# A two-layer decoder trunk on one core: score products over all 128 rows, value products and compression alternating between two column halves

## The chip, the core and the metric

The kernel runs on one core of one Trainium2 chip. The metric is the device time of one execution in microseconds (us). The median of three runs of the kernel before is 717.5 us (716.52 to 721.53).

## What is computed

There are two layers over 256 tokens of width 1024, all in float32. Cut to what matters here, a layer is:

```
h   = RMSNorm(x);  p = h @ W_in                 # one projection, columns split among three groups of heads
o_A = HGRN2 gated linear recurrence             # 4 heads, state 64x64
o_B = gate0*softmax(q.kc)vc + gate1*softmax(q.ks)vs + gate2*softmax(q.kw)vw    # 8 heads of 64, 2 groups of keys
      kc, vc = gelu(flat(32-token blocks of k, v) @ w1) @ w2                   # 15 compressed keys and values a group
o_C = softmax(q.k + c_q - c_k) v                # forgetting attention, 4 heads of 64; c = running sum of log f
x   = x + concat(o_A, o_B, o_C) @ W_o
x   = x + relu(RMSNorm(x) @ W_up)^2 @ W_down
```

With 256 tokens, the selected branch (ks, vs) and the window branch (kw, vw) of B each see every key up to the query's position.

## The kernel before, in words

Every weight matrix streams through one DMA queue (SyncE's, SP) in tiles of 128 x 1024 values (512 KB). `load` (L207) puts a tile into one of five `raw` buffers. `load_split` (L212) divides it into two exact float32r parts: ScalarE (ACT) writes `whi` (L219), VectorE (DVE) writes `wlo = raw - whi` (L220). `mm3` (L223) makes one exact product of three float32r products on TensorE (PE), L225 to L227. The projection of W_in, the output projection W_o and the MLP use it; they are most of PE's work.

Between W_in and W_o stand the three groups of heads. A token tile t is 128 tokens.

- **Scores of B** (`head_b`, L804). For each head and token tile two products are summed in a bank `sc`: L813 over 128 rows (rows 0-63 the hi part of q against the hi part of k, rows 64-127 the lo part of q against hi of k), and L814 over rows 0-63 only (hi of q against `KLB`, the lo part of k). `KLB` is the lower half of a tile `KLO`; 256 columns for tile 0, 512 for tile 1. 8 heads x 2 tiles x 2 layers give 32 such pairs. The softmax follows: DVE masks and takes the maximum (L743), ACT exponentiates (L161), DVE and ACT scale (L751, L749), PE transposes (L828, L833), ACT copies to SBUF (L830, L835).
- **Scores of C** (`head_c`, L858). Per token tile three products: L867 over 128 rows, L868 over rows 64-127 (`KLC`, the upper half of `KLO`), and L869 over the two rows 32h and 32h+1 (`ones_r` against `CC`, which holds the running sums). 4 heads x 2 tiles x 2 layers give 16 such triples.
- **Value products of B** (`pv_b`, L838). One bank takes two heads: head e = 0 writes partitions 0-63 (columns 0-63 of the array), head e = 1 partitions 64-127. All four products of the first head come first, then all four of the second, between two full-width products with the compressed values (`cmp_out`, L842). L850 has 256 columns, L852 has 128. These operands are plain float32, and the trace shows each such product as two passes. There are four per layer. `pv_c` (L883) does the same for C with two products a head.
- **Compression** (`b_compress`, L597). The first product of the compressed keys (w = 0) and values (w = 1): 35 output rows, 128 columns, 16 steps each. Steps w0 and w1 of the order do the keys, w2 and w3 the values, each with its own 512 KB `raw` tile, which is used as loaded and so stays held until the step's last product. Both results stand on partitions 0-34, in different columns.

`ORDER` (L54) writes out the steps of a layer by hand. The framework's scheduler then merges them into a stream per engine, and decides when a tile gets a buffer that is free. PE, DVE, ACT and SP each run their stream in order; an instruction that waits holds up all behind it. The steps that the prediction speaks of are these:

```
"t2", "t3", "vg", "b2", "b1", "w0", "t4", "w1", "cv", "+ai", "w2", "w3", "ai", "t5", "kc", "b0", "+q1", "q1", ...
... "b4", "b5", "b6", "c0", "pb2", "b7", "pb3", "c1", "wo0", "pc0", "wo1", "c3", "wo2", "c2", "pc1", "wo3"
```

Here `b` is head_b, `c` head_c, `w` b_compress, `pb` pv_b, `pc` pv_c, `kc` the rest of the compression, `t` a level of A (L466 on PE, then L475 to L486 on DVE), `+q1` the projection of a chunk and `wo` tiles of the output projection.

Of the kernel before, what the change touches and what calls it, by code (L numbers as in the profile page):

```python
# [10 lines left out]
F32 = mybir.dt.float32  # L11
F32R = mybir.dt.float32r
# [6 lines left out]
P = 128  # L19
# [13 lines left out]
# Column chunks of w_in, in the order in which they are projected.  # L33
# (name, list of (first column, end column))
# [16 lines left out]
# The first three chunks are projected together, token tile 0 first; then the steps of a layer up to the output projection, in the  # L51
# order in which they are issued ("+" marks the projection of a chunk, its bare name the use of the result).
# [6 lines left out]
# Parts of the probabilities that ScalarE scales (0-3: of B, 4-5: of C); VectorE scales the others.  # L59
# buffers of weight tiles: as loaded, their hi parts, their lo parts  # L60
WBUFS = (5, 6, 5)
# [9 lines left out]
# Columns of the constant table.  # L71
# [12 lines left out]
# Columns of the per-layer table of small parameters.  # L84
V_BQG = 0      # per-partition gain of the B queries (1 on the rotary dims)
# [3 lines left out]
V_POS = 4      # [kv, 16]  # L89
# [5 lines left out]
V_LB = V_FB + 4   # [pair, layer]  # L95
V_G2 = V_LB + 4    # per K-tile
# [39 lines left out]
def tile_block(ctx: ExitStack, tc: tile.TileContext, x_in, win, wo, wup, wdn, w1, vec, cst, out, dbg=None):  # L136
# [4 lines left out]
    # One table set holds every activation used here.  # L141
# [13 lines left out]
    def act_exp(*a, **k):  # L155
        """Exp and Ln come from the set loaded last; they stay behind its load."""
        if after[0] is None:
            r = A.activation(*a, **k)
        else:
            with tc.issue_after(after[0]):  # L160
                r = A.activation(*a, **k)  # L161
        last_exp[0] = r.ins
        return r

    def act_sigmoid(*a, **k):
        """Sigmoid comes from another set: behind every Exp and Ln issued so far."""
# [18 lines left out]
    # ---- tiles that live through the whole kernel  # L185
# [6 lines left out]
    ones_r = T([P, P], F32R, tag="ones_r", pool=cpool)  # L192
# [4 lines left out]
    KLO = T([P, 1024], F32R, tag="KLO", pool=cpool)  # L197
# [4 lines left out]
    for z in (Qbd, AT, LF, hidT, KC.bitcast(F32), VC.bitcast(F32), PCS.bitcast(F32)):  # L202
        G.memset(z, 0.0)
    KLB = KLO[0:64, :].rearrange("p (g n) -> p g n", g=2)
    KLC = KLO[64:128, :].rearrange("p (h t) -> p h t", h=4)

# [5 lines left out]
    def load_split(src, n, parts=1):  # L212
        """Loads [128, n] of weights; gives exact float32r parts hi and lo, worked out in so many parts."""
# [23 lines left out]
    def rsqrt(ss, n, a, b, parts=P, st="n", out=None, rms=None):  # L237
        """(a * ss + b) ** -0.5 on [parts, n], with one Newton step. With rms, ss is of unscaled values of both
        token tiles, a names the column of a * r^2, and the result is multiplied by r."""
# [21 lines left out]
    def norm_stats(t):  # L261
        """mean(x^2) + eps of the tokens of tile t."""
# [19 lines left out]
    def kt_split():  # L282
        """Exact parts hi and lo of a [1024, 256] operand, feature-major, four K-tiles a tile."""
        return [[T([P, 4, S], F32R, "kt4", 6) for _ in range(2)] for _ in range(2)]

    def kt_parts(a, k, sl):
        """hi and lo of K-tile k, columns sl."""
# [4 lines left out]
    def gain_splits(a, ks, sl, ps, vt, v0):  # L292
        """K-tiles ks of a, columns sl, from what stands side by side in ps, times their gains."""
# [8 lines left out]
    def begin(L):  # L302
        """Tiles of a layer's start: parameters, x * g1 feature-major, 1 / rms of x, the first tile of w_in."""
# [6 lines left out]
        rms = T([P, 2, 4], tag="rms", bufs=1)    # per token tile: r, r^2, r^2 / DH, -r  # L310
# [3 lines left out]
    def norm1(st, t):  # L314
        """x * g1 of the tokens of tile t, feature-major; 1 / rms goes on what the projections give."""
# [21 lines left out]
    for L in range(DEPTH):  # L337
# [10 lines left out]
        def proj_tok(name):  # L348
            """Token-major projection of 256 columns: one bank, [token tile, 256]."""
# [6 lines left out]
        def proj_feat(name):  # L356
            """Feature-major projection of 256 columns: one bank, [column block, 256 tokens]."""
# [763 lines left out]
```

## Time and profile before

| | us |
|---|---|
| median of the runs shown | 717.5 |
| span of the profiled execution | 715.8 |
| PE busy in the span | 705.0 |
| DVE busy | 453.3 |
| ACT busy | 398.5 |
| POOL (GpSimd) busy | 8.3 |

The profiled execution is listed by its span alone, 715.8 us from its first to its last instruction; the runs' median lies 1.7 us above it, with what stands around the span. L12 is line 12 of the kernel. PEld are the weight loads that overlap products. A product's own time includes its way through the array, so consecutive products overlap in the listing, and what one costs in a stream is the distance from its start to the next start. A wait that is hidden in such an overlapped row is not listed as idle.

### The profile page before, as it was taken

The page shows a single profiled execution, that of the slowest core. Times are in us where ns is not written, and L with a number is a line of the kernel's source. Part 1 is how long each engine was busy: PE and PEld are TensorE (multiplying, and loading weights), DVE is VectorE, ACT ScalarE, POOL GpSimd, SP SyncE. Part 2 cuts the span into 40 slices and gives each one's busy share as a digit, 9 for nine tenths or more (in the row PEclk, how much of TensorE's full clock was granted, in tenths as well). Part 3 has the DMA queues.
Part 4 walks back from the last instruction along what each step waited for, and adds up shares of the span by engine and source line. Part 5 has one row for each costly group of instructions (what it writes and reads, how often), then busy time and mean ns, then how long its engine had stood idle before and what let it go on. Part 6 is the DMA issues. An engine that isn't in the chain of part 4 may idle for free.

```text
span 715.8 us, 11877 instructions
## 1 busy us (share of the span) xinstructions
PE 705.0 (98%) x4578; PEld 619.1 (86%) x4578; DVE 453.3 (63%) x988; ACT 398.5 (56%) x759; POOL 8.3 (1%) x21
## 2 busy tenths in 40 slices
PE   6999999999999999999999999999999999999997
PEld 6998988668988998899799989976689888998896
DVE  5879878727655545555577998685285556545552
ACT  7655666867554444444567456577665445434440
POOL 3000000000100000000000000000000000000000
PEclk9999999999999999999999999899899999999999
DMA  8852632005565565565455436120065565556521
GB/s 321 258 168 71 228 97 90 30 0 179 183 203 179 178 190 190 181 189 178 133 177 201 129 117 208 54 66 30 2 219 191 178 190 193 177 180 196 184 88 60
DMA packets 31017, 108.88 MB, mean 152 GB/s; under 512 B 3568, under 2 KB 4080, under 8 KB 30960
## 3 DMA queue, kind: packets, MB, share of 16 engines
q1 hardware_dynamic: 30960, 108.11, 46.7%
q8 instruction: 36, 0.59, 0.4%
q14 instruction: 21, 0.17, 0.1%
HBM read 107.05 MB, written 1.05 MB: 151 GB/s over the span
## 4 chain that ended last, share of the span: by engine, by line
PE 94%; DVE 3%; DMA 1%; ACT 1%; issue 1%; SPq 0%
PE acc L225 11%; PE acc L227 10%; PE acc L226 10%; PE sc L225 9%; PE sc L226 9%; PE sc L227 9%; PE pv L226 3%; PE pv L225 3%; PE pv L227 3%; PE pa L225 3%; PE pa L227 3%; PE pa L226 3%; PE pv L850 2%; PE sc L605 2%; PE sc L814 2%; PE pa L466 2%
## 5 line engine op out<-in xcount | busy, mean ns | idle before, releaser
L220 DVE TENSOR_TENSOR wlo<-raw,whi 128x1024 fp32r<-128x1024 f32 (+2 forms) x197 | 235.5, 1199 | 133.1 <-PE sc L227 67.1
L219 ACT ACTIVATE whi<-raw 128x1024 fp32r<-128x1024 f32 (+2 forms) x197 | 203.4, 1042 | 189.0 <-PE sc L226 76.9
L225 PE MATMUL sc<-kt,whi 128*128 128x256 f32 x512 | 145.3, 284 | 0.0
L226 PE MATMUL sc<-kt,whi 128*128 128x256 f32 x512 | 144.8, 283 | 0.0
L227 PE MATMUL sc<-kt,wlo 128*128 128x256 f32 x512 | 144.7, 283 | 0.0
L225 PEld LDWEIGHTS sc<-kt,whi 128*128 128x128 f32 x512 | 98.1, 192 | 1.0 <-ACT s L1009 0.3
L226 PEld LDWEIGHTS sc<-kt,whi 128*128 128x128 f32 x512 | 98.1, 192 | 0.6
L227 PEld LDWEIGHTS sc<-kt,wlo 128*128 128x128 f32 x512 | 98.1, 192 | 0.0
L225 PE MATMUL acc<-whi,kt 128*128 128x256 f32 (+2 forms) x288 | 91.7, 318 | 2.5 <-ACT whi L219 2.4
L226 PE MATMUL acc<-wlo,kt 128*128 128x256 f32 (+2 forms) x288 | 88.7, 309 | 0.0
L227 PE MATMUL acc<-whi,kt 128*128 128x256 f32 (+2 forms) x288 | 88.7, 309 | 0.0
L225 PEld LDWEIGHTS acc<-whi,kt 128*128 128x128 f32 x288 | 56.7, 197 | 7.0 <-ACT whi L219 3.0
L227 PEld LDWEIGHTS acc<-whi,kt 128*128 128x128 f32 x288 | 56.2, 195 | 2.9 <-issue 1.1
L226 PEld LDWEIGHTS acc<-wlo,kt 128*128 128x128 f32 x288 | 56.5, 197 | 2.0 <-issue 1.0
L225 PE MATMUL acc<-whi,big 128*128 128x512 f32 x128 | 50.7, 396 | 0.0
L226 PE MATMUL acc<-wlo,big 128*128 128x512 f32 x128 | 50.6, 395 | 0.0
L227 PE MATMUL acc<-whi,big 128*128 128x512 f32 x128 | 50.5, 394 | 0.0
L743 DVE CUSTOM_DVE_ANT_0 big<-sc,cst 128x128 f32<-128x128 f32 (+1 forms) x80 | 27.2, 354 | 26.9 <-PE sc L869 19.8
L161 ACT ACTIVATE big<-big,nmx 128x128 f32<-128x128 f32 (+1 forms) x80 | 35.6, 446 | 14.8 <-DVE nmx L743 14.6
L1010 DVE TENSOR_TENSOR s<-s 128x512 f32<-128x512 f32 x32 | 22.1, 690 | 24.1 <-ACT s L1009 24.1
L1009 ACT ACTIVATE s<-sc 128x512 f32<-128x512 f32 x32 | 18.8, 588 | 18.7 <-PE sc L227 18.7
L227 PEld LDWEIGHTS acc<-whi,big 128*128 128x128 f32 x128 | 24.0, 188 | 5.8
(300 smaller groups left out, 1218.6 us busy)
## 6 DMA issues: line engine op xcount, KB each, us to landing
raw<-in_wup_dram SPq DMA_DIRECT2D x64, 512.0 KB, 3.3
raw<-in_wdn_dram SPq DMA_DIRECT2D x64, 512.0 KB, 3.3
raw<-in_win_dram SPq DMA_DIRECT2D x44, 512.0 KB, 4.1
raw<-in_wo_dram SPq DMA_DIRECT2D x16, 512.0 KB, 4.5
raw<-in_w_dram SPq DMA_DIRECT2D x8, 512.0 KB, 3.6
raw<-in_win_dram SPq DMA_DIRECT2D x4, 426.0 KB, 3.9
out_dram<-x SPq DMA_DIRECT2D x4, 256.0 KB, 2.0
raw<-in_win_dram SPq DMA_DIRECT2D x2, 284.0 KB, 3.0
```

The lines of the kernel that those rows point to most:

```text
L161: r = A.activation(*a, **k)
L219: A.activation(hi[:, c0], raw[:, c0], AF.Copy)
L220: V.tensor_sub(lo[:, c0], raw[:, c0], hi[:, c0].bitcast(F32))
L225: PE.matmul(ps, ah, wh, start=start, stop=False)
L226: PE.matmul(ps, ah, wl, start=False, stop=False)
L227: PE.matmul(ps, al, wh, start=False, stop=stop)
L466: PE.matmul(ps[:, o:o + P].rearrange("p (a b h) -> p a b h", a=2, h=h), Kc[:, p, t * P:(t + 1) * P], mv, start=True, stop=True)
L605: PE.matmul(pre_[0][:35, w * P:(w + 1) * P], zf[:, j:j + 273:8], raw[:, j8 * P:(j8 + 1) * P], start=(j == 0), stop=(j == 15))
L743: V.tensor_tensor_reduce(out=dst, in0=ps, in1=mask, scale=-1.0, scalar=3.0e38, op0=ALU.add, op1=ALU.min, accum_out=nmx)
L814: PE.matmul(ps[:, :n], qS[par][0:64, pair, sl], KLB[:, g, c0:c0 + n], start=False, stop=True)
L1009: A.activation(rl, pu[i], AF.Relu)
L1010: V.tensor_mul(rl, rl, rl)
```

## The change

- `KLO` becomes two full tiles, `KLB` and `KLC`, whose unused 64 rows are zeroed once at the start. L814 and L868 multiply over 128 rows. In L869 the 2-row operand becomes a 128-row one: `sel_r` holds 1 in column h on rows 32h and 32h+1, and is broadcast to 128 columns; all rows of `CC` take part.
- In `pv_b` and `pv_c` the products of the two heads alternate, so the output changes column half with each one.
- In `b_compress` keys and values alternate at each step, the keys' result on partitions 0-34, the values' on 64-98. Steps w0 and w2 load two raw tiles at once. Two copies on ACT take the place of one.
- Five raw buffers become four.

```diff
-WBUFS = (5, 6, 5)
+WBUFS = (4, 6, 5)
...
-    ones_r = T([P, P], F32R, tag="ones_r", pool=cpool)
+    sel_r = T([P, 4], F32R, tag="sel_r", pool=cpool)
-    KLO = T([P, 1024], F32R, tag="KLO", pool=cpool)
+    KLB = T([P, 2, 512], F32R, tag="KLB", pool=cpool)
+    KLC = T([P, 4, S], F32R, tag="KLC", pool=cpool)
...
-    for z in (Qbd, AT, LF, hidT, KC.bitcast(F32), VC.bitcast(F32), PCS.bitcast(F32)):
+    for z in (Qbd, AT, LF, hidT, KC.bitcast(F32), VC.bitcast(F32), PCS.bitcast(F32), KLB[64:128].bitcast(F32),
+              KLC[0:64].bitcast(F32), sel_r.bitcast(F32)):
         G.memset(z, 0.0)
-    KLB = KLO[0:64, :].rearrange("p (g n) -> p g n", g=2)
-    KLC = KLO[64:128, :].rearrange("p (h t) -> p h t", h=4)
+    for h_ in range(4):
+        G.memset(sel_r[32 * h_:32 * h_ + 2, h_:h_ + 1].bitcast(F32), 1.0)
...
-        def b_compress(w, i):
+        raw1 = []
+        def b_compress(i):
             if not pre_:
                 pre_.append(bank("sc"))
-            zf = Z[:, w].rearrange("p g m -> p (g m)")
-            raw = load(w1[L, w, :, i * 1024:(i + 1) * 1024], 1024)
-            for j8 in range(8):
-                j = i * 8 + j8
-                PE.matmul(pre_[0][:35, w * P:(w + 1) * P], zf[:, j:j + 273:8], raw[:, j8 * P:(j8 + 1) * P],
-                          start=(j == 0), stop=(j == 15))
+            if i % 2 == 0:
+                raw1[:] = [load(w1[L, w, :, i * 512:i * 512 + 1024], 1024) for w in range(2)]
+            for j4 in range(4):
+                j, c0 = i * 4 + j4, (i % 2 * 4 + j4) * P
+                for w in range(2):
+                    PE.matmul(pre_[0][64 * w:64 * w + 35, 0:P], Z[:, w].rearrange("p g m -> p (g m)")[:, j:j + 273:8],
+                              raw1[w][:, c0:c0 + P], start=(j == 0), stop=(j == 15))
...
-            A.activation(presb, pre[:35, 0:256], AF.Copy)
...
+                A.activation(presb[:, w * P:(w + 1) * P], pre[64 * w:64 * w + 35, 0:P], AF.Copy)
...
-                PE.matmul(ps[:, :n], qS[par][0:64, pair, sl], KLB[:, g, c0:c0 + n], start=False, stop=True)
+                PE.matmul(ps[:, :n], qS[par][:, pair, sl], KLB[:, g, c0:c0 + n], start=False, stop=True)
...
-            for e_ in range(2):
-                o = po[64 * e_:64 * e_ + 64, :]
-                p0, p1 = PT[g * 4 + jj * 2 + e_]
-                for bi in range(2):
-                    PE.matmul(o[:, 0:S], VS[:, 0, bi * 2 + g, :], p0[:, bi, :], start=False, stop=False)
-                for bi in range(2):
-                    PE.matmul(o[:, P:S], VS[:, 1, bi * 2 + g, :], p1[:, bi, :], start=False, stop=False)
+            for bi in range(2):
+                for t in range(2):
+                    for e_ in range(2):
+                        PE.matmul(po[64 * e_:64 * e_ + 64, t * P:S], VS[:, t, bi * 2 + g, :],
+                                  PT[g * 4 + jj * 2 + e_][t][:, bi, :], start=False, stop=False)
...
-                PE.matmul(ps[:, :n], cqS[e_][64:128, u_, sl], KLC[:, hd, 0:n], start=False, stop=False)
-                PE.matmul(ps[:, :n], ones_r[32 * hd:32 * hd + 2, :], CC[32 * hd:32 * hd + 2, 0:n], start=False, stop=True)
+                PE.matmul(ps[:, :n], cqS[e_][:, u_, sl], KLC[:, hd, 0:n], start=False, stop=False)
+                PE.matmul(ps[:, :n], sel_r[:, hd:hd + 1].to_broadcast([P, P]), CC[:, 0:n], start=False, stop=True)
...
-                PE.matmul(o[:, 0:S], CV[:, 0, hd, :], PTC[hd][:, 0:S], start=True, stop=False)
-                PE.matmul(o[:, P:S], CV[:, 1, hd, :], PTC[hd][:, S:S + P], start=False, stop=True)
+                    PE.matmul(po[64 * e_:64 * e_ + 64, t * P:S], CV[:, t, hd, :], PTC[hd][:, t * S:t * P + S],
+                              start=t == 0, stop=t == 1)
```

Three places show what the scheduler makes of it. Lines of the changed kernel stand 4 to 8 further down here (L605 is L613, L828 is L836, L833 is L841, L842 is L850, L850 and L852 are both L858; L466 is L470, L209 is L213).

On PE, first layer, the first half of the compression stood before as two runs, keys' first tile (`raw_944`), then keys' second (`raw_965`), with a level of A (L466) between:

```order
L828 MATMUL tr_895<-cst_70,big_155_871 128x128 x3
L833 MATMUL tr_902<-cst_70,big_155_871 128x128 x2
L605 MATMUL sc_943<-raw_944,Z_169 35x128 x7
L466 MATMUL pa_954<-Qbd_74,m_40_167 128x128 x4
L605 MATMUL sc_943<-raw_965,Z_169 35x128 x8
L828 MATMUL tr_931<-cst_70,big_165_907 128x128
L225 MATMUL acc_977<-whi_1010,kt_17_94 128x256
```

It now alternates between keys (`raw_951`) and values (`raw_953`):

```order
L836 MATMUL tr_902<-cst_70,big_156_878 128x128 x3
L841 MATMUL tr_909<-cst_70,big_156_878 128x128 x2
L613 MATMUL sc_950<-raw_953,Z_177 35x128
L613 MATMUL sc_950<-raw_951,Z_177 35x128
L613 MATMUL sc_950<-raw_953,Z_177 35x128
L613 MATMUL sc_950<-raw_951,Z_177 35x128
L613 MATMUL sc_950<-raw_953,Z_177 35x128
L613 MATMUL sc_950<-raw_951,Z_177 35x128
```

The products are as many; each now writes the other column half than the one ahead of it.

On PE, first layer, the second head of the third value product of B (`pv_1792`) stood before in two pieces with an output-projection product between (names: `P` probabilities, `VS` values, `tr` transposes):

```order
L850 MATMUL pv_1792<-P_328_1724,VS_172 64x256 x2
L226 MATMUL acc_1880<-wlo_1909,kt_33_160 128x512
L852 MATMUL pv_1792<-P_330_1729,VS_172 64x128 x2
L828 MATMUL tr_1755<-cst_70,big_331_1731 128x128
L842 MATMUL pv_1792<-PCT_1368,VC_80 128x256
```

Its end now is (`pv_1800`):

```order
L836 MATMUL tr_1763<-cst_70,big_332_1739 128x128
L841 MATMUL tr_1770<-cst_70,big_332_1739 128x128
L858 MATMUL pv_1800<-P_329_1732,VS_180 64x256
L858 MATMUL pv_1800<-P_321_1701,VS_180 64x128
L858 MATMUL pv_1800<-P_331_1737,VS_180 64x128
L850 MATMUL pv_1800<-PCT_1376,VC_81 128x256
```

The last three value products of both heads now follow each other; the five ahead of them stand as one, two and two, with transposes and other products between.

On SP, first layer, the DMA issues from the compression's third and fourth tile (`raw` from `in_w`) to the tiles after it were, with the engines that each waits for:

```order
L209 DMA raw_1038<-in_w_dram 128x1024 [waits DMAHW0_49,DVE_49,Activation_49]
L209 DMA raw_1048<-in_w_dram 128x1024 [waits DMAHW3_49,DVE_49]
L209 DMA raw_1165<-in_win_dram 128x1024 [waits DMAHW4_49,DVE_49]
L209 DMA raw_1195<-in_win_dram 128x1024 [waits DMAHW7_49,DVE_49]
L209 DMA raw_1469<-in_win_dram 128x1024 [waits DMAHW1_49,PE_49]
L209 DMA raw_1499<-in_win_dram 128x1024 [waits DMAHW0_49,DMAHW2_49,DVE_49,Activation_49]
L209 DMA raw_1530<-in_win_dram 128x1024 [waits PE_49]
```

They now are:

```order
L213 DMA raw_1045<-in_w_dram 128x1024 [waits DMAHW3_49,DVE_49]
L213 DMA raw_1047<-in_w_dram 128x1024 [waits DMAHW4_49,DVE_49,Activation_49]
L213 DMA raw_1173<-in_win_dram 128x1024 [waits DMAHW1_49,PE_49]
L213 DMA raw_1203<-in_win_dram 128x1024 [waits DMAHW2_49,PE_49]
L213 DMA raw_1477<-in_win_dram 128x1024 [waits DMAHW5_49,PE_49]
L213 DMA raw_1507<-in_win_dram 128x1024 [waits DMAHW6_49,PE_49]
L213 DMA raw_1538<-in_win_dram 128x1024 [waits DMAHW7_49,DVE_49]
```

The two tiles behind the compression's, `raw_1173` and `raw_1203` (the chunk q1), now wait for PE, where `raw_1165` and `raw_1195` waited for DVE.

## Rows read from the trace of the kernel before

**Rows 1.** The page, chain that ended last: shares of the span by engine.
```profile
PE 94%; DVE 3%; DMA 1%; ACT 1%; issue 1%; SPq 0%
```

**Rows 2.** Windows, first layer: us, then busy us of PE, PEld, DVE, ACT, POOL; clock, DMA.
```profile
63.40:83.50 20.10, 20.05 (x148) 17.21 (x148) 17.53 (x58) 12.46 (x32) 0.00 (x0) 1.00 0.34 108
83.50:122.90 39.40, 39.38 (x298) 35.12 (x298) 32.44 (x118) 25.79 (x67) 0.00 (x0) 1.00 0.39 133
122.90:160.20 37.30, 37.30 (x172) 24.33 (x171) 18.93 (x84) 26.98 (x86) 0.00 (x0) 0.95 0.08 27
```

**Rows 3.** Timeline of PE: a B score pair among 512-column products (start us, us).
```profile
127.00 0.28 PE L813 MATMUL sc<-KS,qS 128*128 128x256 f32 x1
...
127.86 0.39 PE L226 MATMUL acc<-wlo,kt 128*128 128x512 f32 x1
128.09 0.39 PE L227 MATMUL acc<-whi,kt 128*128 128x512 f32 x1
```

**Rows 4.** Timeline of PE: the scores of one C head and what follows.
```profile
135.48 0.22 PE L867 MATMUL sc<-CK,m 128*128 128x128 f32 x1
...
137.07 0.50 PE L227 MATMUL acc<-whi,kt 128*128 128x512 f32 x1
137.41 0.38 PE L833 MATMUL tr<-cst,big 128*128 128x128 f32 x2
```

**Rows 5.** Timeline of PE and its loads: one unbroken value product of B.
```profile
116.01 1.08 PE L850 MATMUL pv<-P,VS 128*64 128x256 f32 x4
...
116.93 0.27 PE L852 MATMUL pv<-P,VS 128*64 128x128 f32 x1
...
117.85 0.60 PE L852 MATMUL pv<-P,VS 128*64 128x128 f32 x4
...
118.38 0.38 PE L842 MATMUL pv<-PCT,VC 96*128 96x256 f32 x1
...
118.60 0.28 PE L225 MATMUL acc<-whi,kt 128*128 128x256 f32 x1
118.60 0.19 PEld L226 LDWEIGHTS acc<-wlo,kt 128*128 128x128 f32 x1
118.72 0.28 PE L226 MATMUL acc<-wlo,kt 128*128 128x256 f32 x1
```

**Rows 6.** Timeline of PE: a value product of C.
```profile
159.41 0.66 PE L888 MATMUL pv<-P,CV 128*64 128x256 f32 x4
...
159.90 0.39 PE L889 MATMUL pv<-P,CV 128*64 128x128 f32 x4
...
160.22 0.55 PE L877 MATMUL tr<-cst,big 128*128 128x128 f32 x3
```

**Rows 7.** Timeline of PE: second half of the compression, and what follows.
```profile
77.60 0.33 PE L828 MATMUL tr<-cst,big 128*128 128x128 f32 x1
...
79.83 3.72 PE L605 MATMUL sc<-raw,Z 128*35 128x128 f32 x32
83.48 1.16 PE L466 MATMUL pa<-Qbd,m 128*128 128x128 f32 x8
...
84.81 0.39 PE L225 MATMUL acc<-whi,kt 128*128 128x256 f32 x1
```

**Rows 8.** Windows, second layer, columns as in rows 2: two stretches at half clock.
```profile
452.40:459.50 7.10, 7.10 (x30) 6.15 (x30) 4.19 (x23) 1.88 (x7) 0.00 (x0) 0.52 0.04 17
500.40:507.10 6.70, 6.70 (x20) 4.35 (x20) 1.41 (x7) 3.74 (x15) 0.00 (x0) 0.50 0.00 0
```

**Rows 9.** Tile raw from 60 to 90 us: splits (ns min/median/max), DMA to landing.
```profile
L220 DVE TENSOR_TENSOR wlo<-raw,whi x6: 1218/1224/1226, 60.6 to 87.9; 128x1024 fp32r<-128x1024 f32 x6
L219 ACT ACTIVATE whi<-raw x6: 1044/1058/1062, 65.1 to 88.1; 128x1024 fp32r<-128x1024 f32 x6
...
DMA to landing us min/median/max: 3.3/4.7/6.6
```

**Rows 10.** Timeline of POOL at the start.
```profile
0.73 0.95 POOL L203 MEMSET Qbd<- 128x1024 f32 x1 [0.29 <-POOLq L1112]
```

More of the change, by code (lines that the diff above doesn't have):

```diff
@@ L580, in b_keys @@
                     A.activation(KS[64 * i:64 * i + 64, g, :], src, AF.Copy, scale=gcol)
-                V.scalar_tensor_tensor(KLB[:, g, :], src, gcol, KS[0:64, g, :].bitcast(F32), ALU.mult, ALU.subtract)
+                V.scalar_tensor_tensor(KLB[0:64, g, :], src, gcol, KS[0:64, g, :].bitcast(F32), ALU.mult, ALU.subtract)
         qS = [T([P, 4, S], F32R, "qS", 2) for i in range(2)]
@@ L697, in c_keys @@
             ckv = CK.rearrange("p (i a) t -> p a i t", a=2)
-            klv = KLC.rearrange("p (i a) t -> p a i t", a=2)
+            klv = KLC[64:128].rearrange("p (i a) t -> p a i t", a=2)
             for a in range(2):
@@ L884, in pv_c @@
             po = bank("pv")
-            for e_ in range(2):
-                hd = u_ * 2 + e_
-                o = po[64 * e_:64 * e_ + 64, :]
-                PE.matmul(o[:, 0:S], CV[:, 0, hd, :], PTC[hd][:, 0:S], start=True, stop=False)
-                PE.matmul(o[:, P:S], CV[:, 1, hd, :], PTC[hd][:, S:S + P], start=False, stop=True)
+            for t in range(2):
+                for e_ in range(2):
+                    hd = u_ * 2 + e_
+                    PE.matmul(po[64 * e_:64 * e_ + 64, t * P:S], CV[:, t, hd, :], PTC[hd][:, t * S:t * P + S],
+                              start=t == 0, stop=t == 1)
             pv_evac(po, 6 + u_)
@@ L913, in tile_block @@
             V.tensor_copy(hm.rearrange("p a b -> p (a b)"), hm_raw[:, 0:320])
-            V.tensor_copy(ones_r, cs[:, C_ONE:C_ONE + P])
         pss = [bank("acc"), bank("acc"), bank("pv")]
@@ L952, in tile_block @@
         step = {
-            "t": a_level, "w": lambda i: b_compress(i // 2, i % 2), "kc": b_compressed, "a_out": a_out,
+            "t": a_level, "w": b_compress, "kc": b_compressed, "a_out": a_out,
             "cb": b_cmp_branch, "b": lambda i: head_b(i // 4, i % 4), "pb": lambda i: pv_b(i // 2, i % 2),
```

## The prediction

> **What bounds the kernel now.** I read the chain that ended last first: 94% of it is PE, 3% DVE, 1% ACT [rows 1]. Then the windows, cut where the changed products stand. In the first layer PE is busy in practically all of each stretch [rows 2]: from 63.4 to 83.5 us (scores of heads b2 and b1, the compression), from 83.5 to 122.9 (b0, b3, the first two value products of B) and from 122.9 to 160.2 (heads b4 to b7, all of C, the last two). In the same rows DVE is busy 17.53 of 20.1 us, then 32.44 of 39.4, and ACT 26.98 of 37.3 in the last. So PE sets the end, but the first stretch leaves DVE only 2.6 us of air and the last leaves ACT 10.3. Those are the caps on what a faster PE can give. Third came the timeline of PE, for the distance from start to start, as busy rows overlap.
>
> **Scores of B.** L813 starts at 127.00, its partner L814 behind it; then comes a 512-column product, and the next one starts at 127.86 [rows 3]. Among its own kind such a 512-column product takes 127.86 to 128.09, 0.23 us. A 256-column one of full height takes 118.60 to 118.72, 0.12 [rows 5]. As full-height products the three would take 0.12 + 0.12 + 0.23 = 0.47 instead of 0.86: 0.39 goes, although no column less is multiplied. It is the price of going from 128 rows to 64 and back. 32 pairs x 0.39 = 12.5 us of PE. The 512-column pairs are taken alike. If the price stayed at the neighbour wherever a transpose follows, 0.29 a pair would be left, 9.3 us.
>
> **Scores of C.** One head's six products last from 135.48 to 137.07, 1.59 us, and the 512-column product behind takes 0.34 (to 137.41) instead of 0.23 [rows 4]. Six full-height products at 0.12 are 0.72, so 1.59 + 0.11 - 0.72 = 0.98 a head, 7.8 us for eight. The 128-column form among full-height neighbours is not shown alone: between half the 256-column price, 0.06, and all of it, 0.12; I take 0.12, which errs against the change. The ends are 9.3 and, with a quarter of the price kept, 5.8. The broadcast weights of `sel_r` have no row. They load 128 columns like any other load, 0.19 us beside the product before [rows 5], and I cost them so. If the repeated read did not hide, 16 loads would add 3 us.
>
> **Compression.** The second half, 32 passes, lasts from 79.83 to 83.48, 3.65 us or 0.114 a pass [rows 7]. There are 128 passes in the kernel, 14.6 us. Does alternating the column half let two run side by side? C's value product already shows it: its two heads write the two halves with two products each, and its eight passes, four of 256 columns and four of 128, end within 159.41 to 160.22, 0.81 us [rows 6]. By the prices of the unbroken B product, 0.23 for a 256-column pass (116.01 to 116.93 for four) and 0.13 for a 128-column one (117.85 to 118.38 for four) [rows 5], one after the other they would take 1.44. So side by side is what this array does, at 0.56 of the serial time. Halving the compression gives 7.3 us; with 0.56 it is 6.4. I take 7, with 0 as the lower end. `pv_c` itself gains nothing, being there already.
>
> **Value products of B.** The unbroken product has 8 passes of each width, serial 8 x 0.23 + 8 x 0.13 = 2.88, and takes 2.37 (116.01 to 118.38) [rows 5], so only its middle overlaps. At 0.56 it takes 1.6: 0.75 goes. The later ones are cut into pieces by transposes, before and after; the order of PE shows one, two, two and three products for the third, where the single one has no partner. I take 0.7 for each of eight, 5.6 us; the ends are 0 and half of 2.88, 11.5.
>
> PE's own time thus falls by 12.5 + 7.8 + 7 + 5.6 = 32.9 us.
>
> **What of it reaches the end.** Per layer:
> - First stretch: 4 pairs (1.6) and the compression (3.5) make 5.1, but DVE has 2.6 of air. I take 2.5. Before 63.4 nothing is changed.
> - Second: 4 pairs and two value products, 1.6 + 1.4 = 3.0; DVE has 7 us of air, but it and PE hand work to each other. I take 2.5.
> - Third: 8 pairs, half of C's 7.8 and two value products, 3.1 + 3.9 + 1.4 = 8.4, under ACT's 10.3. The chain from a score through DVE, ACT and back to the transposes gets tight, so 7.5.
>
> That is 12.5 a layer, 25 in all.
>
> **Clock.** In the second layer PE's clock is 0.52 and 0.50 (the level of 1.2 GHz, where 1.00 is 2.4) in stretches of 7.1 and 6.7 us [rows 8], both right after work with many switches and narrow products; they lose some 6.8 us. The third stretch of the first layer has a mean of 0.95 [rows 2], 1.9 us lost. The rows of after should be denser there, but PE will wait for others more often. I count 3 us back; the ends are all 8.7 back, or 5 more lost.
>
> **One raw buffer less.** In the dense stages a tile is needed every 24 products of 0.12, 2.9 us, and a raw buffer turns over in a landing of 4.7 us (median, 3.3 to 6.6) and the splits, 1.06 and 1.22 [rows 9], some 7 us; four buffers then give a tile every 1.75 us. That hides it. At the compression it does not: all four buffers hold its tiles, and SP's order shows q1's two loads waiting for PE to finish the first half. From there to q1's first product (L225) before leaves 77.60 to 84.81, 7.2 us [rows 7], less the 1.8 that the faster second half saves: 5.4 us. Issue, landing and split take 3.3 + 2.3 = 5.6 at best and 8.9 at worst. So PE waits between 0.2 and 3.5 us a layer; I take 1, near the best, as the queue is empty there: 2 us lost.
>
> **The rest.** Two zeroed half tiles of 1024 columns (0.95 us each by Qbd's row) run on POOL in the first microseconds [rows 10], while KLB is first read by a score of B, and the earliest of these stand at the head of the stretch from 63.4; POOL does nothing from there on [rows 2]. The second copy on ACT in `b_compressed` has a level of A between on PE. Cost 0; without that cover some 0.4 a layer.
>
> **Sum.** 25 + 3 - 2 = 26 us off the profiled span of 715.8 gives 689.8; the runs' median lies 1.7 above that span, so **691.5 us**.
>
> **A rule of the skill against it.** In rows 5 the load of L226 starts at 118.60 and takes 0.19, while L225 runs over the same rows, and its product starts 0.12 later: loads run ahead though the rows are the same. The Trainium skill (TensorE: Matmul & The Clock Gate, Part 3: Packing small matmuls — row/col tiling) says that weight loads overlap running products only when their row groups differ. By that, products made full height would each pay their load, rival D below; the trace disagrees.
>
> **Rivals.**
> - A, PE takes all of it: DVE and ACT keep up, so 32.9 + 5 - 1 = 37 us go, 680. For it: in the last stretch DVE is busy only 18.93 of 37.3 us. Against it: DVE's 17.53 of 20.1 in the first.
> - B, others take over: the first two stretches give nothing, and in the last ACT, which is busy 26.98, stays 5 us behind: 5 a layer, no clock back, 10 - 2 = 8 off, 709.
> - C, slower: alternating does not overlap but empties the array at each change of half, at the 0.2 us that a change of height costs (half of 0.39). 64 changes in the compression and 64 in B's value products cost 26 us, and the overlap that B's products have now, 0.5 each, is lost, 4 more; against 20.3 from the scores that is 10 slower, 727. It decides from (20.3 - 4)/128 = 0.13 us a change. Against it: C's value product [rows 6] changes half without such a price. The Trainium skill (TensorEngine Tiling (Array Packing), Key Properties) says that changing the mode drains the engine, but not changing the tile; rows 6 agree with the second half.
> - D, full height doesn't pay: each of the 64 products that grew (32 + 16 + 16) shows its 0.19 load. 64 x 0.19 = 12 given back: 703.
>
> **Chances.** Forecast 0.58 (681 to 702), A 0.18, B 0.13, D 0.06, C 0.03, and 0.02 for something unnamed. The range 677 to 707 reaches A's end with some clock, and most of the way to B. A measurement of this kernel tells about 1% from no change, 710.3 us being the border: faster 0.92 (B's upper tail is left out), same 0.05, slower 0.03.
>
> **What would show it.** Right: L813 to L814 and on at 0.12 and 0.23, no gap at C's third product; the second half of the compression within about 2 us; the four unbroken rows of a value product within 1.6. New waits of PE should name DVE in the first stretch and ACT in the last, and one of about 1 us for q1's `whi` behind the compression. Wrong: PE's changed rows as long as before (C or D), waits of PE of more than 15 us in all (B), or none (A).

## The result: 698.56 us, and the profile after

The changed kernel takes 698.56 us (median of 4 runs, 696.44 to 699.29) against 717.75 (4 runs, 716.52 to 721.53): ratio 0.973, 95% interval 0.9693 to 0.9766, 19.2 us less. The forecast was 691.5 us, range 677 to 707: faster, as forecast, with 26 us named and 19 found. Times of the runs further down leave out four slow ones, each more than 1.5% above the fastest of its kernel: 721.22 us of the kernel before, 737.70 and 738.54 of e7, and 1658.11 of e12, for which nothing on record shows a cause.

The page of the changed kernel (span, busy times, the chain that ended last):

```profile
span 697.3 us, 11902 instructions
...
PE 675.9 (97%) x4578; PEld 602.4 (86%) x4578; DVE 451.6 (65%) x987; ACT 398.0 (57%) x761; POOL 10.9 (2%) x28
...
PE 82%; DVE 8%; ACT 5%; DMA 3%; issue 1%; SPq 0%; ACTq 0%
```

PE's share of the chain is 82%, where it was 94% [rows 1]; DVE has 8%. The span can be split in three by the page and by the mean clock of the core (0.988 before, 0.993 after): what PE is not busy; what the clock takes, span x (1 - clock); and the rest, PE's work at full clock.

| us of the profiled span | before | after | change |
|---|---|---|---|
| span | 715.8 | 697.3 | -18.5 |
| PE not busy (span - busy) | 10.8 | 21.4 | +10.6 |
| lost to the clock | 8.6 | 4.9 | -3.7 |
| PE's work at full clock | 696.4 | 671.0 | -25.4 |

The last row is good to some 4 us only: by it, five runs with the same products on PE (the changed kernel, e4, e5, e9 and e12) come out between 666.6 and 671.0.

The changed products first, in the timeline of PE. A pair of B's scores, and half a head of C (start, us, as in rows 3):

```profile
138.14 0.28 PE L821 MATMUL sc<-KS,qS 128*128 128x256 f32 x1
138.26 0.28 PE L822 MATMUL sc<-KLB,qS 128*128 128x256 f32 x1
138.37 0.40 PE L231 MATMUL acc<-whi,kt 128*128 128x512 f32 x1
...
146.01 0.39 PE L874 MATMUL sc<-CK,m 128*128 128x256 f32 x1
146.23 0.28 PE L875 MATMUL sc<-KLC,m 128*128 128x256 f32 x1
146.36 0.28 PE L876 MATMUL sc<-CC,sel_r 128*128 128x256 f32 x1
146.48 0.40 PE L229 MATMUL acc<-whi,kt 128*128 128x512 f32 x1
```

138.14, 138.26, 138.37: 0.12 a product, and no gap at the 512-column product behind, where the pair of [rows 3] with its neighbour stood 0.39 longer. C's three 256-column products lie 0.22, 0.13 and 0.12 apart; the first pays for the value product of B ahead of it. The product with the broadcast weights costs what any other does. The second half of the compression, then an unbroken value product of B and one of C:

```profile
77.81 1.98 PE L613 MATMUL sc<-raw,Z 128*35 128x128 f32 x32
79.72 1.16 PE L470 MATMUL pa<-Qbd,m 128*128 128x128 f32 x8
```

```profile
120.00 1.52 PE L858 MATMUL pv<-P,VS 128*64 128x256 f32 x16
121.45 0.39 PE L850 MATMUL pv<-PCT,VC 96*128 96x256 f32 x1
```

```profile
157.06 0.87 PE L895 MATMUL pv<-P,CV 128*64 128x256 f32 x8
157.86 0.50 PE L231 MATMUL pa<-whi,kt 128*128 128x512 f32 x1
```

32 compression passes take 1.91 us, 0.060 each instead of 0.114 [rows 7]; B's sixteen 1.45 us instead of 2.37 [rows 5]; C's eight 0.80, as before [rows 6]. So each edit does what it says.

The windows of the first layer, cut at the same products as in [rows 2] (columns as there):

```profile
63.70:79.72 16.02, 15.49 (x150) 13.89 (x149) 13.73 (x55) 9.00 (x29) 0.00 (x0) 1.00 0.20 66
79.72:118.70 38.98, 35.54 (x257) 33.17 (x256) 32.11 (x107) 25.65 (x62) 0.00 (x0) 0.91 0.49 149
118.70:157.90 39.20, 38.54 (x239) 26.65 (x237) 24.46 (x103) 34.61 (x104) 0.00 (x0) 1.00 0.13 41
```

The first stretch is 16.0 us instead of 20.1, the second 39.0 instead of 39.4: there PE stands idle for 38.98 - 35.54 = 3.4 us, and the mean clock is 0.91, another 3.5. (The third is no shorter because more of the dense products now fall into it, 239 products on PE instead of 172.) Who PE waits for (us in all, times, longest):

```profile
PE sc L640 <- DVE hidT L638: 2.7, 2, 1.5
PE acc L229 <- ACT whi L223: 2.7, 2, 2.4
PE sc L772 <- DVE KC L659: 2.3, 2, 1.1
...
PE tr L841 <- ACT P L838: 1.4, 2, 0.7
PE tr L652 <- DVE s L552: 0.8, 2, 0.4
```

The wait forecast for q1 is hardly there: of the 2.7 us of L229, 2.4 are the start's, as before, and q1's first products show some 0.2 us in the timeline of PE:

```profile
81.06 0.38 PE L229 MATMUL acc<-whi,kt 128*128 128x256 f32 x1
81.43 0.39 PE L230 MATMUL acc<-wlo,kt 128*128 128x256 f32 x1
81.66 0.28 PE L231 MATMUL acc<-whi,kt 128*128 128x256 f32 x1
```

The second starts when DVE's split of q1's first tile ends (81.38). Instead PE waits for links of one chain on DVE, the compressed keys (L638, L552, L659). The chain of waits from 76 to 106 us shows why (start, us, what):

```profile
80.24 6.14 DMA raw<-in_win_dram
86.40 1.07 ACT whi L223
87.49 1.23 DVE wlo L224
...
89.30 1.16 DVE wlo L224
90.46 0.13 DVE hidT L638
...
98.96 0.69 DVE sA L517
99.79 1.14 DVE wlo L224
100.92 0.14 DVE s L544
...
103.52 1.13 DVE wlo L224
104.68 0.25 DVE KC L659
104.98 1.04 PE sc L772 x4
```

This tile is not q1's but one of the chunk behind it: the fourth of the loads behind the compression, and it lands 6.14 us after its issue (q1's two, issued at 75.31 and 75.73, took 3.73 and 4.53). Its split (L224) and the next tile's stand ahead of L638 in DVE's queue, and more splits stand ahead of L544 and L659. SP's waits from 55 to 100 us and DVE's from 60 to 106 us show where that began:

```profile
SPq L213 <- PE sc L613: 20.3, 2, 16.7
```

```profile
DVE wlo L224 <- ACT whi L223: 3.0, 2, 2.0
```

The last load of a compression tile is issued at 58.44 us in SP's timeline, the next load of any tile at 75.31, once PE has done the first half: for 16.7 us no raw buffer is free. Then six loads go out within 9 us. DVE stands idle 2.0 us for the first of them and 1.05 for the fourth, and has their splits to do when the key chain is due. What follows on PE, by windows:

```profile
100.00:104.80 4.80, 2.76 (x20) 2.01 (x18) 4.77 (x16) 4.52 (x14) 0.00 (x0) 1.00 0.37 110
104.80:111.60 6.80, 6.62 (x29) 6.34 (x30) 4.21 (x25) 1.97 (x7) 0.00 (x0) 0.50 0.27 77
```

PE is busy 2.76 of 4.80 us, and the clock is 0.50, its lower level, in the 6.8 us behind.

### The profile page after: what moved, and what is told of

It is laid out like the page before. It is cut to its first block, busy times and chain, and to the rows that moved or that the text cites. A ratio compares the mean times of both kernels' runs of the same rounds, so it can differ in the third digit from the quotient of the medians.

```text
span 697.3 us, 11902 instructions
## 1 busy us (share of the span) xinstructions
PE 675.9 (97%) x4578; PEld 602.4 (86%) x4578; DVE 451.6 (65%) x987; ACT 398.0 (57%) x761; POOL 10.9 (2%) x28
## 3 DMA queue, kind: packets, MB, share of 16 engines
HBM read 107.05 MB, written 1.05 MB: 155 GB/s over the span
## 4 chain that ended last, share of the span: by engine, by line
PE 82%; DVE 8%; ACT 5%; DMA 3%; issue 1%; SPq 0%; ACTq 0%
PE sc L229 9%; PE sc L230 9%; PE sc L231 9%; PE acc L229 9%; PE acc L231 8%; PE acc L230 8%; PE pv L230 3%; PE pv L231 3%; PE pv L229 3%; DMA raw<-in_win_dram 3%; PE pa L231 3%; PE pa L230 3%; PE pa L229 3%; DVE wlo L224 2%; PE pv L858 2%; PE sc L613 1%
## 5 line engine op out<-in xcount | busy, mean ns | idle before, releaser
L224 DVE TENSOR_TENSOR wlo<-raw,whi 128x1024 fp32r<-128x1024 f32 (+2 forms) x197 | 235.2, 1197 | 139.1 <-PE sc L231 67.2
L229 PE MATMUL sc<-kt,whi 128*128 128x256 f32 x512 | 145.1, 283 | 0.0
L229 PEld LDWEIGHTS sc<-kt,whi 128*128 128x128 f32 x512 | 98.0, 191 | 1.0 <-ACT s L1015 0.3
L229 PE MATMUL acc<-whi,kt 128*128 128x256 f32 (+2 forms) x288 | 88.9, 309 | 2.7 <-ACT whi L223 2.7
L231 PE MATMUL acc<-whi,kt 128*128 128x256 f32 (+2 forms) x288 | 88.4, 309 | 0.2
L229 PEld LDWEIGHTS acc<-whi,kt 128*128 128x128 f32 x288 | 56.8, 197 | 5.3 <-ACT whi L223 3.3
L229 PE MATMUL acc<-whi,big 128*128 128x512 f32 x128 | 50.7, 396 | 0.0
L161 ACT ACTIVATE big<-big,nmx 128x128 f32<-128x128 f32 (+1 forms) x80 | 35.6, 447 | 16.4 <-DVE nmx L751 16.3
```

The source lines that it names most:

```text
L224: V.tensor_sub(lo[:, c0], raw[:, c0], hi[:, c0].bitcast(F32))
L229: PE.matmul(ps, ah, wh, start=start, stop=False)
L231: PE.matmul(ps, al, wh, start=False, stop=stop)
```

## The experiments

Executions of one kernel differ mostly by the clock. The kernel before, run 50 times beside the experiments, took 709.86 us with a clock of 1.000 and 719.23 with 0.986; span x clock lies between 705.8 and 708.6 in every one of them. So the table gives, beside the time, the median over the runs of span x clock, the span at full clock. Within one of the other kernels it scatters by up to 4.0 us (e9), so differences of 1 or 2 us between two rows mean little.

| kernel | us (runs) | ratio to before, 95% interval | clock of the runs | span at full clock |
|---|---|---|---|---|
| before | 717.75 (4) | | 0.983 to 1.000 (50) | 707.0 (50) |
| after | 698.56 (4) | 0.973 (0.9693 to 0.9766) | 0.990 to 0.995 | 690.9 |
| e1, scores at 64 rows | 711.59 (12) | 0.9948 (0.9922 to 0.9973) | 0.987 to 0.994 | 704.5 |
| e2, values head by head | 705.07 (6) | 0.9861 (0.9822 to 0.99) | 0.990 to 0.995 | 698.6 |
| e3, compression in blocks | 697.42 (6) | 0.9756 (0.9717 to 0.9794) | 0.990 to 0.995 | 690.8 |
| e4, keys first | 698.83 (6) | 0.9789 (0.9736 to 0.9842) | 0.980 to 0.998 | 691.0 |
| e5, five raw buffers | 691.99 (6) | 0.9676 (0.9638 to 0.9715) | 0.991 to 0.995 | 684.8 |
| e6, compression of before | 704.05 (6) | 0.9846 (0.9802 to 0.9891) | 0.988 to 0.992 | 696.0 |
| e7, before with four raw | 727.62 (4) | 1.0186 (1.0122 to 1.0249) | 0.972 to 0.995 (6) | 717.5 (6) |
| e8, e6 with five raw | 688.64 (6) | 0.963 (0.9592 to 0.9669) | 1.000 | 686.5 |
| e9, joint loads | 697.04 (6) | 0.9742 (0.9701 to 0.9784) | 0.989 to 0.995 | 689.9 |
| e10, e9 with five raw | 692.87 (5) | 0.9681 (0.9641 to 0.9721) | 0.992 to 0.993 | 685.9 |
| e11, before, five high | 708.38 (5) | 0.9896 (0.9855 to 0.9937) | 0.999 to 1.000 | 706.1 |
| e12, after, five high | 697.56 (5) | 0.977 (0.9724 to 0.9817) | 0.987 to 0.990 | 688.3 |

**One part undone at a time (e1 to e3).** e1 gives the second and third products of a score their old heights:

```diff
-PE.matmul(ps[:, :n], qS[par][:, pair, sl], KLB[:, g, c0:c0 + n], ...)
+PE.matmul(ps[:, :n], qS[par][0:64, pair, sl], KLB[0:64, g, c0:c0 + n], ...)
...
-PE.matmul(ps[:, :n], cqS[e_][:, u_, sl], KLC[:, hd, 0:n], ...)
-PE.matmul(ps[:, :n], sel_r[:, hd:hd + 1].to_broadcast([P, P]), CC[:, 0:n], ...)
+PE.matmul(ps[:, :n], cqS[e_][64:128, u_, sl], KLC[64:128, hd, 0:n], ...)
+r_ = slice(32 * hd, 32 * hd + 2)
+PE.matmul(ps[:, :n], sel_r[r_, hd:hd + 1].to_broadcast([2, P]), CC[r_, 0:n], ...)
```

> The changed kernel with the second products of the scores back at 64 rows and the third of C at 2 rows; the zero rows stay allocated, all else as in the changed kernel. Theory 1 (the price of the height, counted from start to start at full clock: the score rows took 34.3 us before and take 20.6 in the changed kernel; PE sets the end where these stand): 11 to 14 of these 13.7 us come back, 709.5 to 712.5 us. Theory 2 (the changed kernel waits for VectorE and ScalarE 10 us longer; a slower PE only eats these waits): under 8 us come back, 703 to 706. In either case the pairs L821/L822 lie at 0.3 to 0.4 us from start to start instead of 0.21.

Two pairs in its timeline:

```profile
126.02 0.40 PE L821 MATMUL sc<-KS,qS 128*128 128x512 f32 x1
126.35 0.49 PE L822 MATMUL sc<-KLB,qS 64*128 64x512 f32 x1
126.77 0.38 PE L821 MATMUL sc<-KS,qS 128*128 128x256 f32 x1
127.08 0.38 PE L822 MATMUL sc<-KLB,qS 64*128 64x256 f32 x1
127.39 0.50 PE L229 MATMUL acc<-whi,kt 128*128 128x512 f32 x1
```

The four products take 1.37 us where four full-height ones of these widths take 0.70. At full clock 704.5 - 690.9 = 13.6 us come back (13.0 in time): theory 1. By its page (span 708.3, busy 690.7, clock 0.994) PE's work is 686.5, 15.5 more than after (to the 4 us said above), and its time out of work falls by 3.8 us, from 21.4 to 17.6.

e2 puts the loop over heads outside again in `pv_b`:

```diff
-for bi in range(2):
-    for t in range(2):
-        for e_ in range(2):
+for e_ in range(2):
+    for t in range(2):
+        for bi in range(2):
```

> The changed kernel with B's value products in the order of before, one head after the other. Theory 1 (start to start the 128 products took 21.5 us before and 16.3 after, at full clock, and PE sets the end there): 4 to 5.5 us come back, 702.5 to 704 us, and the unbroken row takes about 2.4 us instead of 1.5. Theory 2 (waits of PE for ScalarE near them eat it): at most 2 us, 698 to 700.5.

```profile
119.02 2.43 PE L858 MATMUL pv<-P,VS 128*64 128x256 f32 x16
```

2.43 us for the unbroken row, as before; 7.7 us come back at full clock (6.5 in time). Theory 1, and more than its 4 to 5.5; start to start the products of B take 22.8 us in e2 and 16.3 after, so 6.5 of it are their own, and the rest is within the scatter. e3 turns two loops of `b_compress`, so that four products write one column half, then four the other:

```diff
-for j4 in range(4):
-    for w in range(2):
+for w in range(2):
+    for j4 in range(4):
```

> The changed kernel with the compression in blocks of four products on one column half, then four on the other; the loads and held buffers as in the changed kernel. Theory 1 (two products overlap only where neighbours write different halves): a pass goes from 0.06 back to 0.10 us or more, 4 to 6 us of PE in all, of which about half reaches the end because VectorE fills that stretch: 700.5 to 702. Rival 1 (all of it reaches the end): 703 to 705. Rival 2 (the overlap needs only that both halves are in use within a group): passes stay near 0.06, 698 to 699.5.

```profile
77.04 2.60 PE L613 MATMUL sc<-raw,Z 128*35 128x128 f32 x32
79.58 1.16 PE L470 MATMUL pa<-Qbd,m 128*128 128x128 f32 x8
```

2.54 us for 32 passes, 0.079 each, between the two rates; over 128 passes 2.4 us more of PE. Nothing of it reaches the end (690.8 against 690.9). The time, 697.42, comes nearest to rival 2's, but not by its mechanism: PE's time out of work falls from 21.4 to 18.0 us in its place (span 695.0, busy 677.0), and its wait of 2.7 us for L638 is gone from its list. So the loss is hidden in a wait behind DVE.

**Order or buffer (e4, e5, e12).** The scheduler of the changed kernel had put A's output ahead of the compressed keys. e4 issues it behind them:

```diff
+kc_last[:] = [kc_pe.ins, kc_v.ins]      # last transpose and last DVE step of the compressed keys
...
+with tc.issue_after(kc_last[0]), tc.issue_after(kc_last[1]):
     a_out()
```

> The changed kernel with A's output products and sums issued behind the compressed keys on PE and VectorE, as they stood before the change. Theory 1 (the scheduler's new order is what PE waits for: VectorE stands with A's sum at 98.96 us ahead of the key chain; waits of 2.2 us a layer for L652, L841 and L772, and behind them the half clock of 104.8 to 111.6): 2 x 2.2 plus most of the 5.0 us lost to the clock go, 690 to 693.5 us. Theory 2 (VectorE is full there, so any order makes PE wait): the wait moves to another row, 697 to 700. Theory 3 (the late raw tiles of q1, one buffer less, are the cause): little changes, 697 to 699, and the key chain still ends behind 103 us.

```profile
PE tr L654 <- DVE s L552: 5.6, 2, 2.8
```

691.0 at full clock: no change. The wait of L652 (now L654) grew from 0.8 to 5.6 us: four splits still stood ahead of the chain in DVE's queue. Theory 1, the order, falls. The time fits theories 2 and 3 alike; the wait moved to another row, as theory 2 had it, and the key chain ends at 101.1 us, where theory 3 had it behind 103. e5 and e12 change one line, `WBUFS` (raw, high, low), from (4, 6, 5) to (5, 5, 5) and (4, 5, 5):

> The changed kernel with five raw buffers again, and one buffer of the split's high half less in exchange (5, 5, 5 instead of 4, 6, 5), as memory holds no more. Theory H (the compression holds all four raw buffers, the tiles behind it land late, and VectorE, which stood idle 3.0 us for them between 60 and 106 us, then has four splits in its queue ahead of the key chain for which PE waits): the waits of PE for L638, L552 and L659 shrink from 5.8 us to under 3, 692 to 695.5 us. Theory D (VectorE is full in that stretch whatever the buffers): 697 to 700, the waits as long.

> The changed kernel with five buffers of the high half instead of six, raw buffers four as in the changed kernel. It tells apart what made the run with five raw buffers 6.6 us faster. If the raw buffer: 697 to 700 us here, PE idle for 20 us or more of the span as in the changed kernel. If the buffer given in exchange (its lack alone made the kernel before 8.6 us faster): 690 to 693.5 us, and the idle time falls to 18 us or less.

With five raw buffers DVE's wait for the tile, in the view shown above, shrinks from 3.0 us to

```profile
DVE wlo L224 <- ACT whi L223: 0.6, 2, 0.3
```

and the time falls to 691.99; PE's waits for L638, L552 and L659 are gone from its list, others on DVE (2.8 us for L544, 1.4 for L778) have come. With four, and the same five of the high half (e12), it is 697.56 us, PE not busy for 20.9 us of the span (18.2 in e5). The buffer is worth 3.5 us at full clock, 5.6 in time: theory H, with part of the wait staying. The buffer given in exchange is worth nothing: without it the span at full clock is even 2.6 us shorter.

But SP stands still just as long with five buffers. Its longest wait for PE in e5:

```profile
SPq L213 <- PE sc L613: 20.9, 2, 17.2
```

What the fifth buffer changes is what goes out ahead of that wait: in e5 one tile of W_in is issued at 56.94 us and lands at 60.35, the next at 74.35; in the changed kernel and in e12 none goes out until 75.31 and 74.44.

**The buffer without the change (e7, e11).**

```diff
-WBUFS = (5, 6, 5)
+WBUFS = (4, 6, 5)
```

> The kernel before with four raw buffers instead of five, nothing else. The forecast's step (a tile each 1.75 us from four buffers against one each 2.9 us needed; the compression gives its tiles back one by one): within 1.5 us of the kernel before. Rival (the fifth buffer is what keeps the loads ahead through the dense stages): 3 to 6 us slower than before.

717.5 at full clock (all six runs), 10.5 us more; in time 727.62 (four runs, 724.22 to 734.43, further apart than any other), 11.7 more than the 715.92 of the kernel before beside it. DVE's waits for `whi` in the same 46 us, 0.9 before, and the longest new waits of PE:

```profile
DVE wlo L220 <- ACT whi L219: 4.5, 3, 2.5
```

```profile
PE pa L491 <- DVE m L483: 2.3, 2, 1.4
PE sc L764 <- DVE KC L651: 2.1, 2, 1.1
```

They name the same key chain (L651) and its neighbours as in the changed kernel. Neither theory's number: the buffer costs more than the rival's 3 to 6, and PE's longest new waits are not for tiles but behind DVE. Here too SP's long wait for PE is there with five buffers and with four (12.5 us at the longest in the kernel before, 16.5 in e11, 16.0 in e7), and the loads ahead of it are what differs: two tiles of q1 go out before it in the kernel before, at 54.18 and 61.80 us, one in e11 (57.48), none in e7 until 74.62. e11 takes (5, 5, 5):

> The kernel before with five buffers of the high half instead of six, five raw: what the buffer that was given in exchange costs by itself. If the exchange is free, within 1.5 us of the kernel before; if the high half is as tight as the raw tiles, 5 us or more slower.

At full clock 706.1, 0.9 less than the kernel before: the exchange is free. Yet the time is 708.38, 8.7 us less than the 717.04 of the kernel before beside it, nearly all of it clock. Where [rows 8] has 0.52:

```profile
450.00:460.00 10.00, 10.00 (x78) 9.20 (x77) 8.12 (x35) 7.61 (x19) 0.00 (x0) 1.00 0.17 51
```

**The compression (e6, e8 to e10).** e6 puts the old compression into the changed kernel, with four raw buffers; e8 the same with (5, 5, 5). e9 keeps the alternation but has one load bring 512 columns of both kinds into one buffer, so that none is held; e10 the same with (5, 5, 5):

```diff
-if i % 2 == 0:
-    raw1[:] = [load(w1[L, w, :, i * 512:i * 512 + 1024], 1024) for w in range(2)]
+raw = T([P, 1024], F32, "raw", WBUFS[0], wpool)
+nc.sync.dma_start(raw.rearrange("p (w c) -> p w c", w=2),
+                  w1[L, :, :, i * 512:i * 512 + 512].rearrange("w p c -> p w c"))
...
-                              raw1[w][:, c0:c0 + P], start=(j == 0), stop=(j == 15))
+                              raw[:, w * 512 + c0:w * 512 + c0 + P], start=(j == 0), stop=(j == 15))
```

> The changed kernel with the whole compression as before the change: keys, then values, a raw tile loaded for each half and given back at once. Its products take 6.5 us longer by their own rows. The forecast's step (half of the compression's gain reaches the end): 701 to 702.5 us. Theory H (what PE gains there is lost in waits behind it, and the loads that are held cost as much): 695 to 699.

> Compression as before and five raw buffers with five of the high half: of the change only the score products and B's value products are left. Theory H: as fast as the better of the two runs above or better, 692 to 697. The forecast's step (the compression's gain half reaches the end, a raw buffer is worth 1 us a layer): 699 to 701.

> The changed kernel, four raw buffers, its products in the same alternation of the column halves; but a load brings 512 columns of the keys' weights and 512 of the values' into one raw buffer, which is given back after its eight products, where the changed kernel holds four buffers. Theory H (holding the buffers is what the compression's gain was paid with): clearly under the changed kernel, 691 to 696 us, and under the run with the compression of before at four buffers by its own 6 us or more. Theory N (with four buffers the loads come late in any case, and the compression's part is hidden): 697 to 704, between those two.

> The same with five raw buffers and five of the high half. Theory H: the 3.4 us by which the held buffers made the alternated compression slower than the old one at five buffers turn into a gain, 683 to 687.5 us. Theory N (the compression lies in a stretch that VectorE fills, its gain is hidden): 688 to 690, as the old compression.

With four buffers the old compression costs 5.1 us at full clock against the changed kernel, 6.1 against e9: the forecast's step, above its 3.5, and theory H missed. Joint loads gain 1.0, within the scatter of the runs (687.7 to 691.7 against 689.3 to 692.4): holding the buffers was not the main price, having four of them was. That is the first half of theory N; its second half, that the compression's part is hidden, fails, as theory H's 6 us against e6 came. In e9 SP waits 14.5 us for PE and sends no tile of q1 ahead of that, as in the changed kernel. With five, the old compression (686.5) is behind the alternating ones (684.8 and 685.9) by 1.7 and 0.6 only; most of the gain is hidden. In time e8 came out below both of its expectations and e10 above both of its own, the one with a clock of 1.000, the other with 0.993.

In time e8 is the fastest of all, 688.64 us, ahead of both kernels, because it keeps its clock in all six runs. From 90 to 106 us PE hardly waits and the clock is 1.00 (window):

```profile
90.00:106.00 16.00, 15.97 (x125) 14.89 (x125) 12.56 (x55) 10.82 (x32) 0.00 (x0) 1.00 0.32 100
```

## Why the prediction was right, and where it was not

In spans at full clock there are two paths from one kernel to the other. By e7 and e6: 707.0, a raw buffer less 717.5, scores and value products 696.0, compression 690.9. By e11, e8, e5 and e12: five high buffers 706.1, products 686.5, compression 684.8, a raw buffer less 688.3, six high buffers 690.9. The clock stands beside both: 717.75 - 707.0 = 10.75 and 698.56 - 690.9 = 7.66, so 3.1 back. The forecast's 25 falls into some 3.4 for the compression (its 3.5 of the first stretch's 5.1, of which 2.5 were to reach the end, twice) and 21.6 for the products.

| term, us | forecast | by e7, e6 | by e11, e8, e5, e12 |
|---|---|---|---|
| scores and value products | -21.6 | -21.5 | -19.6 |
| compression | -3.4 | -5.1 | -1.7 |
| one raw buffer less | +2 | +10.5 | +3.5 |
| one high buffer less and back | | | -0.9 + 2.6 |
| clock | -3 | -3.1 | -3.1 |
| sum | -26 | -19.2 | -19.2 |

- **The step that failed is "One raw buffer less".** It saw that q1's loads would wait for PE, and priced one wait: PE's, for q1's first product, 0.2 to 3.5 us, of which it took 1. That wait came at its lower end, some 0.2 us at 81.43, as q1's tiles landed after 3.73 and 4.53 us. The price lay elsewhere. DVE paid, idle 3.0 us and then behind with the splits of the loads that left late, and its next chain, the compressed keys, was late: PE waits 5.8 us for its links (L638, L552, L659). Nothing was counted for what stands behind a late split in DVE's queue, or for the clock after such a wait. Its price hangs on the compression beside it. The same exchange of buffers, five raw and five high against four and six, costs 9.5 us with the old compression (e8, e6), 6.1 with the new one (e5, after) and 4.0 with joint loads (e10, e9). On the first path the raw buffer is more than the whole distance of 6.8 us between forecast and result; on the second 1.5 of it, and the products, the compression and the high buffer, which no step had, are 1.7 to 2.0 each. In time, the changed kernel with the fifth buffer (e5) takes 691.99.
- **Scores: right mechanism, too high a price.** 12.5 + 7.8 = 20.3 us were taken. Start to start at full clock, B's 64 products fell from 22.0 to 13.6 us over the whole trace and C's 48 from 12.3 to 7.0, 13.7 together, and 13.6 come back at the end in e1, nearly all. PE's work in e1, 15.5, is the rougher measure. Two things were too high: the neighbour's 0.1 us was counted with every pair and head, and after the change a pair takes 0.42 us on average, where the full-height prices of [rows 3] and [rows 5] give 0.35, and a head of C 0.88 instead of 0.72. Why these are above the cleanest rows is not shown.
- **Value products: 5.6 taken.** Start to start they fell from 21.5 to 16.3 us, 5.2; at the end 7.7 came back in e2, with a scatter of some 3 us on either side. The unbroken row takes 1.45 us, forecast "1.6". (The upper end of 11.5 takes 1.44 off each product, but an unbroken one, at 2.37, would lose 0.93 if its serial 2.88 were halved.)
- **Compression: 7 taken from PE,** 6.5 measured start to start (15.2 to 8.7 us); the forecast let half of it reach the end. With four buffers 5.1 did, with five 0.6 to 1.7. So a cap shows only where the loads are early; that it is DVE's, as forecast, is argued and not tested.
- **The end's share.** 25 of 32.9 us were to reach the end. Start to start, the four kinds of products together fell by 25.4 (8.4 + 5.3 + 5.2 + 6.5), and the three parts, undone one by one with four buffers, give 13.6 + 7.7 + 5.1 = 26.4. Too high a work and too careful a cap cancelled: that the 25 is so near is luck.
- **Clock: 3 taken, 3.1 measured,** and this too is luck. The 3 was a guess between 8.7 back and 5 lost, without saying which stretch would win or lose. The profiled kernel before is at 0.50 in stretches of 3.4, 6.8 and 6.8 us, the changed one in a new stretch of 6.8, behind its waits, and in one of 3.4. With the median of the 50 runs of the kernel before, 716.32, in place of the first four, the term is 1.6.
- **Rivals.** A (no cap at all) comes near for the products, but its 37 us needed the full 32.9 of work. B, 709 us, is out: what e1 and e2 undo comes back nearly whole. Its sign did show: the listed waits of PE add up to 17.1 us, more than the 15 of the forecast (7.0 before), so that sign did not tell B apart. The new waits name DVE, as forecast, but in the second stretch and not in the first; ACT has 0.3 us in the last. C is out: a pass that changes the column half takes 0.060 us, less than the 0.114 before. D is out: the products at 138 and 146 us are 128 rows high and 0.12 apart, less than a load's 0.19 [rows 5]. The list of what overlaps in the Trainium skill (TensorE: Matmul & The Clock Gate, Part 3: Packing small matmuls — row/col tiling) would have each load wait for its predecessor on the same rows; the trace after disagrees as the one before did.

What stays open: five raw and six high buffers beside the zero-padded tiles don't fit the memory, so the buffer's price in the changed kernel itself wasn't tried, only that with five high ones. Each change of a buffer count also lets the scheduler merge the streams anew: a high buffer less made the changed kernel 2.6 us faster at full clock, so as much of any price in the table may be a matter of order, and no run holds the order while it changes the buffers. What decides whether a run keeps its clock is not settled either.

## What to carry to other kernels

Price a buffer taken from a ring by the loads that no longer go out ahead of a stretch in which all the others are held: that stretch was as long with five buffers (e5, e11) as with four, but with four at least one tile less went ahead of it. Then follow it past the first consumer to what is queued behind that on the engine that splits or converts the tile. On PE, products of lower height among full ones cost more than their zero rows would, and alternating column halves shortens narrow ones (here 0.060 us a pass instead of 0.114, and 1.45 instead of 2.37 for a value product); read the price from several places, not from the cleanest one. Compare variants by span x clock as well as by time: 9 us between two runs of one kernel here are the clock's alone.

## What was not expected of the hardware

The same program took 709.86 or 719.23 us with nothing but the granted clock between (1.000 and 0.986; span x clock 708.1 and 707.4), while e8 and e11 kept 0.999 to 1.000 in all of their 11 runs. The lower level (0.50 in the rows at 104.8 us) came behind a stretch in which PE waited in the changed kernel, but in the kernel before PE was busy all through the 12.4 us ahead of it, from 440.0 to 452.4, and in the stretch itself [rows 8]. And four products per column half already bring two thirds of the overlap: 0.114 us a pass on one half, 0.079 in blocks of four, 0.060 one by one.
